# Value and gate products of a two-layer trunk: 256 weight columns a pass at 180 bytes, or 512 at 108 bytes

## The chip, the core and the metric

The kernel runs on one core of a Trainium2 chip. Its time is the device time of one execution in microseconds (us); the time before is the median of three runs. The profile is one further execution, recorded by the hardware profiler. In its rows PE is the matrix engine, PEld the load of its stationary tile, DVE the vector engine, ACT the scalar engine, POOL the general one, SP the engine that issues most transfers.

## The reference

The reference is a trunk of two layers on 256 tokens of width 2048, all in float32:

```python
for i in range(DEPTH):
    h = rms_norm(x, mixer_norm[i])
    if i % N_MIXERS == 0:
        x = x + diff_attention(h, ...)      # h @ w_qkv, scores, softmax, values, @ w_o
    else:
        x = x + gated_deltanet(h, ...)      # h @ w_in, convolution, delta rule, gate z, @ w_out
    x = x + conv_ffn(rms_norm(x, ffn_norm[i]), ...)   # @ w_up, convolution, gate, @ w_down
return x
```

Nearly all of the work is products of 256 tokens with large weights, each weight used once. Two groups of them matter here: the value columns of the attention, `v = h @ w_qkv[:, 4096:6144]`, and the gate columns `z` of the gated DeltaNet, 4096 columns of `h @ w_in`.

## The kernel before

**Three products for one.** Every float32 operand of a large product is split into two parts in the type fp32r, `hi` and the remainder `lo`, and the product is hi·hi + lo·hi + hi·lo, three matmuls accumulated into the same PSUM tile. The activations are kept split in SBUF: `h` holds, for each of the 16 blocks of 128 input features, 256 columns of `hi` and then 256 of `lo`.

**Weights.** `weights` (L78) fetches a piece of 1024 columns, 512 KB, on SP's queue into `raw`, ACT copies it to `whi` (L89), DVE subtracts to get `wlo` (L90). `raw`, `whi` and `wlo` have three buffers each, so a copy to `whi` waits until PE has finished the piece three before. The tiles `whi` and `wlo` are 1024 + 128 elements long, and the second argument of `weights` says at which element of the first 128 the data starts.

**Two kinds of product.** `dense` (L101) has the weight as the stationary tile, 128 x 128, and the activations as the moving one, 256 tokens wide: L115 to L117. It makes 19,344 of the kernel's 23,504 matmuls. `dense_tok` (L125) turns this round, as its result is wanted with the tokens on the partitions: the stationary tile is 128 feature rows by 128 tokens of `h`, the moving one is 512 columns of weight, sent as two halves of 256 (L139). It is called four times with `w_v` (L399) and eight times with `w_z` (L687). Each call goes through 16 blocks `k` of features in 8 pieces of two; for each block it goes over the two halves `c` of the tokens, the three products `j`, and the two halves of the columns: 24 matmuls a piece, 192 a call, 2304 in all. The result has a PSUM tile of two banks, `ps[:, c, :]`, 512 columns each; `dps` holds two such tiles. ACT takes the result out of PSUM, at L402 for v and at L689 for z.

**Placement.** `HP`, `AP`, `OP` are the columns, modulo 128 elements (512 bytes), at which the rows of `h`, of the FFN's activations and of the mixer's output start. `dense` places its weights 45 elements (`GAP`) ahead of that, `dense_tok` 45 elements behind it, so that in both the moving tile starts 180 bytes past the stationary one modulo 512.

**Order.** At the end of each piece `tick` (L73) advances a list of generators by one step each: these do the small work beside the products, such as scores and softmax of the attention during `w_qk` and `w_v`, and during `w_z` the inversion of the delta rule's triangular matrices (`invert`, L512: 30 rounds of two small DVE instructions, L525 and L528, a step each three rounds; then two transposes, L532 and L534, on which PE's L553 waits). `total` (L221) sums squares by a matmul with a tile of ones (L226), with 512 moving columns of fp32r for q and k. The Tile scheduler may move instructions on each engine; each engine then runs its own in order. In layer 1 the calls with `w_z` come in pairs, four pairs in all; `dense` with `w_in` follows each.

Of the kernel before, what the change touches and what calls it, by code (L numbers as in the profile page):

```python
# [16 lines left out]
P = 128  # L17
T = 256
# [1 line left out]
KD = D // P  # L20
EPS = 1e-6
CK = 4
GAP = 45
HP, AP, OP = 40, 48, 112
LNEXP = "natural_log_exp_and_others"

# [1 line left out]
class Trunk:  # L28
# [72 lines left out]
    def dense(self, w, kt, acts, place, tiles=2, lead=0):  # L101
# [3 lines left out]
        for k0, nk in self.chunks(kt, CK, lead):  # L105
            hi, lo = self.weights(w[:, k0:k0 + nk, :], (place - GAP) % P)
            steps = [(k, c) for k in range(nk) for c in range(tiles)]
# [17 lines left out]
    def dense_tok(self, w, kt, acts):  # L125

        nc = self.nc
        ps = self.banks()
        for k0, nk in self.chunks(kt, CK // 2):
            hi, lo = self.weights(w[:, k0:k0 + nk, :], (HP + GAP) % P)  # L130
            for k in range(nk):
                a = acts(k0 + k)
                first, last = k0 + k == 0, k0 + k == kt - 1
                for c in range(2):
                    ah, al = (a[:, i, c * P:(c + 1) * P] for i in range(2))
                    halves = [slice(i * T, (i + 1) * T) for i in range(2)]
                    for j, (l, r) in enumerate(((ah, hi), (ah, lo), (al, hi))):
                        for i, s in enumerate(halves):
                            nc.tensor.matmul(ps[:, c, s], l, r[:, k, s],  # L139
                                             start=first and not (i or j), stop=last and i + j == 3)  # L140
            self.tick()
        return ps

# [764 lines left out]
```

## Time and profile before

| | |
|---|---|
| Median of 3 runs | 2675.52 us (2675.1 to 2675.8) |
| The profiled execution | 2676.33 us, of which its span is 2674.6 us |
| Mean granted clock of TensorE | 0.999 |
| PE, 23,504 matmuls | 2656.4 us busy |
| DVE / ACT / POOL busy | 1845.2 / 1453.3 / 112.1 us |
| HBM read | 476.03 MB, 179 GB/s over the span |

Read it so: a row of the timeline or of a group gives the start in us, the duration, the engine, the line of the kernel, the operation, what it writes and reads, the shape, and how many instructions are merged in it. Matmuls overlap in the pipeline, so the duration of one (some 280 ns for 256 columns) is not what it costs: the cost is the distance from its start to the start of the next. A row x4 at 210.36 followed by a row at 210.84 says that four matmuls cost 0.48 us. A small part of the matmul records can be missing.

### The profile page before, as it was taken

Reading aid. Unit: us, or ns where it says so; the run is one execution under the profiler, and the core shown is the slowest. Engines: PE = TensorE matmul, PEld = TensorE weight load, DVE = VectorE, ACT = ScalarE, POOL = GpSimd, SP = SyncE. Lnnn points to the kernel's source line nnn. Section 1 sums busy time; section 2 is a strip of 40 time slices with the busy share of each in tenths; the row PEclk is TensorE's granted clock in tenths of the full one; section 3 lists DMA queues with packets and bytes.
Section 4 is the critical chain, followed back from the end, with each engine's and each line's share of the span. In section 5 each row is a group of like instructions: output and inputs, shape, how many; then the busy total and the mean of one; then the engine's idle time right before and its main releaser. Section 6 shows DMA issues by size and latency. Waiting matters only on the chain.

```text
span 2674.6 us, 55978 instructions
## 1 busy us (share of the span) xinstructions
PE 2656.4 (99%) x23504; PEld 2639.4 (99%) x23504; DVE 1845.2 (69%) x2719; ACT 1453.3 (54%) x1994; POOL 112.1 (4%) x221
## 2 busy tenths in 40 slices
PE   8999999999999999999999999999999999999999
PEld 8999999999999999999999999999999999999999
DVE  7775567777777555688787687688677777776444
ACT  6555555555555444584764664574565555554333
POOL 0000000000000000031011021021000000000000
PEclk9999999999999999999999999999999999999999
DMA  6555566666666666655355454555466666666765
GB/s 205 172 174 164 159 192 194 195 195 193 195 193 195 193 194 192 190 156 177 115 170 166 143 169 155 157 159 174 143 194 195 194 193 196 193 195 197 203 200 165
DMA packets 135469, 481.77 MB, mean 180 GB/s; under 512 B 15408, under 2 KB 18480, under 8 KB 135216
## 3 DMA queue, kind: packets, MB, share of 16 engines
q1 hardware_dynamic: 134064, 475.58, 58.6%
q8 instruction: 184, 3.01, 0.5%
q10 hardware_dynamic: 1152, 2.61, 0.3%
q14 instruction: 69, 0.57, 0.1%
HBM read 476.03 MB, written 2.10 MB: 179 GB/s over the span
## 4 chain that ended last, share of the span: by engine, by line
PE 93%; DVE 3%; ACT 3%; issue 1%; DMA 1%; ACTq 0%; DVEq 0%; SPq 0%
PE ps L115 26%; PE ps L116 26%; PE ps L117 26%; PE ps L139 10%; PE mp L610 2%; DVE wlo L90 1%; ACT whi L89 1%; PE mp L226 1%; DVE cv L207 1%; ACT L455 0%; PE mp L574 0%; PE mp L580 0%; DMA raw<-w_in 0%; PE mp L589 0%; PE mp L498 0%
## 5 line engine op out<-in xcount | busy, mean ns | idle before, releaser
L90 DVE TENSOR_TENSOR wlo<-raw,whi 128x1024 fp32r<-128x1024 f32 (+2 forms) x909 | 1105.2, 1217 | 660.9 <-ACT whi L89 659.8
L89 ACT CAST whi<-raw 128x1024 fp32r<-128x1024 f32 (+2 forms) x909 | 948.6, 1044 | 1034.8 <-PE ps L117 830.8
L115 PE MATMUL ps<-h,whi 128*128 128x256 f32 x4304 | 1195.0, 278 | 7.8 <-ACT h L152 5.6
L116 PE MATMUL ps<-h,wlo 128*128 128x256 f32 x4304 | 1194.8, 278 | 4.4 <-DVE wlo L90 4.4
L117 PE MATMUL ps<-h,whi 128*128 128x256 f32 x4304 | 1193.7, 277 | 0.0
L115 PEld LDWEIGHTS ps<-h,whi 128*128 128x128 f32 x4304 | 809.4, 188 | 9.8 <-ACT h L152 5.6
L116 PEld LDWEIGHTS ps<-h,wlo 128*128 128x128 f32 x4304 | 809.8, 188 | 7.7 <-DVE wlo L90 5.9
L117 PEld LDWEIGHTS ps<-h,whi 128*128 128x128 f32 x4304 | 810.0, 188 | 0.6
L115 PE MATMUL ps<-ac,whi 128*128 128x256 f32 x1632 | 450.4, 276 | 0.0
L116 PE MATMUL ps<-ac,wlo 128*128 128x256 f32 x1632 | 450.3, 276 | 0.0
L117 PE MATMUL ps<-ac,whi 128*128 128x256 f32 x1632 | 450.2, 276 | 0.0
L115 PEld LDWEIGHTS ps<-ac,whi 128*128 128x128 f32 x1632 | 306.2, 188 | 0.0
L116 PEld LDWEIGHTS ps<-ac,wlo 128*128 128x128 f32 x1632 | 306.2, 188 | 0.0
L117 PEld LDWEIGHTS ps<-ac,whi 128*128 128x128 f32 x1632 | 306.2, 188 | 0.0
L139 PE MATMUL ps<-whi,h 128*128 128x256 f32 x1536 | 251.1, 284 | 0.0
L139 PEld LDWEIGHTS ps<-whi,h 128*128 128x128 f32 x1536 | 213.5, 190 | 0.2
L139 PE MATMUL ps<-wlo,h 128*128 128x256 f32 x768 | 155.7, 284 | 1.0 <-DVE wlo L90 1.0
L115 PE MATMUL ps<-oc,whi 128*128 128x256 f32 x512 | 143.9, 281 | 0.0
L207 DVE SCALAR_TENSOR_TENSOR cv<-u,fcols,cv 128x255 f32<-128x255 f32 (+1 forms) x344 | 142.8, 477 | 0.0
L117 PE MATMUL ps<-oc,whi 128*128 128x256 f32 x512 | 142.5, 278 | 0.0
L116 PE MATMUL ps<-oc,wlo 128*128 128x256 f32 x512 | 142.3, 278 | 0.0
L139 PEld LDWEIGHTS ps<-wlo,h 128*128 128x128 f32 x768 | 119.4, 190 | 2.0 <-DVE wlo L90 1.4
(201 smaller groups left out, 2048.7 us busy)
## 6 DMA issues: line engine op xcount, KB each, us to landing
raw<-w_up SPq DMA_DIRECT2D x344, 512.0 KB, 4.3
raw<-w_down SPq DMA_DIRECT2D x160, 512.0 KB, 4.1
raw<-w_in SPq DMA_DIRECT2D x128, 512.0 KB, 4.1
raw<-w_z SPq DMA_DIRECT2D x64, 512.0 KB, 4.4
raw<-w_out SPq DMA_DIRECT2D x64, 512.0 KB, 3.9
raw<-w_qk SPq DMA_DIRECT2D x63, 512.0 KB, 4.0
raw<-w_v SPq DMA_DIRECT2D x32, 512.0 KB, 3.7
raw<-w_o SPq DMA_DIRECT2D x32, 512.0 KB, 4.1
```

The source lines that it names most:

```text
L89: nc.scalar.copy(hi, raw)
L90: nc.vector.tensor_tensor(lo, raw, hi.bitcast(F32), ALU.subtract)
L115: nc.tensor.matmul(o, hi[:, k, s], a[:, 0, :], start=first, stop=False)
L116: nc.tensor.matmul(o, lo[:, k, s], a[:, 0, :], start=False, stop=False)
L117: nc.tensor.matmul(o, hi[:, k, s], a[:, 1, :], start=False, stop=last)
L139: nc.tensor.matmul(ps[:, c, s], l, r[:, k, s], start=first and not (i or j), stop=last and i + j == 3)
L207: nc.vector.scalar_tensor_tensor(out[:, j:], u[:, :T - j], taps[n - 1 - j], out[:, j:], ALU.mult, ALU.add)
L226: last = self.nc.tensor.matmul(out, self.onesr, p[:, j], start=i + j == 0, stop=i + j == n)
L610: nc.tensor.matmul(p[:, v, :], l(v), r[:, v, :], start=i == 0, stop=i == len(terms) - 1)
```

## The change

`dense_tok` sends the 512 columns of a block in one matmul in place of two. The first and last flags of the accumulation now go by product alone. The data in `whi` and `wlo` starts at element 40 + 27 = 67 in place of 85, so that the moving tile lies 27 elements, 108 bytes, past the stationary tile modulo 512 bytes. The tiles' sizes, the pieces, the transfers, the copies, the ticks and `dense` with its 180 bytes stay as they are.

```diff
-GAP = 45
+GAP, LEAD = 45, 27
...
-            hi, lo = self.weights(w[:, k0:k0 + nk, :], (HP + GAP) % P)
+            hi, lo = self.weights(w[:, k0:k0 + nk, :], HP + LEAD)
             for k in range(nk):
                 a = acts(k0 + k)
                 first, last = k0 + k == 0, k0 + k == kt - 1
                 for c in range(2):
                     ah, al = (a[:, i, c * P:(c + 1) * P] for i in range(2))
-                    halves = [slice(i * T, (i + 1) * T) for i in range(2)]
                     for j, (l, r) in enumerate(((ah, hi), (ah, lo), (al, hi))):
-                        for i, s in enumerate(halves):
-                            nc.tensor.matmul(ps[:, c, s], l, r[:, k, s],
-                                             start=first and not (i or j), stop=last and i + j == 3)
+                        nc.tensor.matmul(ps[:, c, :], l, r[:, k, :], start=first and not j, stop=last and j == 2)
```

## Prediction

> **What bounds the kernel now.** First the page, for its span, its busy engines and the chain that ended last:
>
> ```profile
> span 2674.6 us, 55978 instructions
> ...
> PE 2656.4 (99%) x23504; PEld 2639.4 (99%) x23504; DVE 1845.2 (69%) x2719; ACT 1453.3 (54%) x1994; POOL 112.1 (4%) x221
> ...
> PE 93%; DVE 3%; ACT 3%; issue 1%; DMA 1%; ACTq 0%; DVEq 0%; SPq 0%
> PE ps L115 26%; PE ps L116 26%; PE ps L117 26%; PE ps L139 10%; PE mp L610 2%; DVE wlo L90 1%; ACT whi L89 1%; PE mp L226 1%; DVE cv L207 1%; ACT L455 0%; PE mp L574 0%; PE mp L580 0%; DMA raw<-w_in 0%; PE mp L589 0%; PE mp L498 0%
> ```
>
> PE carries the chain from end to end; the changed line, L139, is 10% of it, about 267 us. Next, who keeps PE waiting:
>
> ```profile
> PE ps L115 <- ACT h L152: 5.6, 1, 5.6
> PE ps L116 <- DVE wlo L90: 4.4, 6, 1.4
> ...
> PE ps L139 <- DVE wlo L90: 1.0, 1, 1.0
> ```
>
> L139 waits 1.0 us in all, and the two rows above it are the largest waits in the kernel. So PE is bound by its own rate, and a nanosecond less for each matmul of L139 comes straight off the end, unless a new wait takes it back. The question is what one matmul costs. The view of line L139, and the timeline of PE, where the distances between starts are what counts:
>
> ```profile
> L139 PEld LDWEIGHTS ps<-whi,h x1536: 186/192/194, 206.3 to 1823.2; 128*128 128x128 f32 x192
> L139 PE MATMUL ps<-whi,h x1536: 278/282/373, 206.4 to 1823.3; 128*128 128x256 f32 x192
> ...
> L139 PE MATMUL ps<-wlo,h x768: 278/285/471, 209.4 to 1823.1; 128*128 128x256 f32 x192
> ...
>   ACT whi L89: 96.4, 64
> ```
>
> ```profile
> 210.12 0.40 PE L139 MATMUL ps<-wlo,h 128*128 128x256 f32 x2
> 210.36 0.64 PE L139 MATMUL ps<-whi,h 128*128 128x256 f32 x4
> ...
> 214.44 0.40 PE L139 MATMUL ps<-wlo,h 128*128 128x256 f32 x2
> 214.68 0.41 PE L139 MATMUL ps<-whi,h 128*128 128x256 f32 x2
> 214.92 0.40 PE L226 MATMUL mp<-sqp,onesr 128*128 128x512 f32 x1
> 215.16 0.28 PE L139 MATMUL ps<-whi,h 128*128 128x256 f32 x1
> 215.27 0.39 PE L226 MATMUL mp<-sqp,onesr 128*128 128x512 f32 x1
> 215.50 0.28 PE L139 MATMUL ps<-whi,h 128*128 128x256 f32 x1
> ```
>
> From 210.12 to 214.44 lie six rounds of six matmuls: 4.32 us / 36 = 120 ns each, so **240 ns for the pair** that makes 512 columns. There are 1536 + 768 = 2304 of them: 2304 x 120 ns = 276 us, which the chain's 10% bears out. Each comes with a load of its own, also 120 ns from one to the next, that takes 192 ns, so every load is under way while the matmul before it streams.
>
> The same view holds the best witness for the new shape: L226 sends 512 columns of the same type in one matmul, 0.24 us before the next start at 214.92, 0.23 us at 215.27. And `dense`, with 256 columns and the same 180 bytes as L139, has two rates:
>
> ```profile
> 1228.83 0.28 PE L115 MATMUL ps<-h,whi 128*128 128x256 f32 x1
> ...
> 1251.86 0.28 PE L115 MATMUL ps<-h,whi 128*128 128x256 f32 x1
> 1252.07 0.69 PE L553 MATMUL mp<-tcc,lt 32*32 32x32 f32 x32
> ...
> 1253.38 0.28 PE L115 MATMUL ps<-h,whi 128*128 128x256 f32 x1
> ...
> 1255.42 0.28 PE L115 MATMUL ps<-h,whi 128*128 128x256 f32 x1
> ```
>
> Directly behind the `w_z` products it runs 64 rounds of three in 23.03 us, 119.9 ns a matmul; after a short break for L553 it runs six rounds in 2.04 us, 113.3 ns. Line, tiles and addresses' rule are the same before and after the break. So the 6.6 ns are no matter of placement alone: PE seems to carry a lag between loads and matmuls along until something lets it catch up. With 256 columns a load has hardly more room than it needs; with 512 it has twice as much.
>
> **The change, part by part.**
>
> *Removed and put in their place:* 1152 matmuls and 1152 stationary loads go, and 1152 matmuls grow from 256 to 512 columns. What does a 512 cost in a row of such? No row shows it, so bounds:
>
> ```profile
> 240.28 0.60 PE L373 MATMUL mp<-aT,v 128*128 128x256 f32 x2
> 240.71 0.38 PE L374 MATMUL mp<-aT,v 128*128 128x128 f32 x2
> ```
>
> ```profile
> L373 PE MATMUL mp<-aT,v x32: 377/379/382, 240.3 to 322.1; 128*128 128x256 f32 x32
> ...
> L374 PE MATMUL mp<-aT,v x32: 271/274/275, 240.7 to 322.4; 128*128 128x128 f32 x32
> ```
>
> ```profile
> 1147.90 0.66 PE L226 MATMUL mp<-qp,onesr 128*128 128x512 f32 x2
> 1148.39 0.29 PE L115 MATMUL ps<-h,whi 128*128 128x256 f32 x1
> ```
>
> Plain float32 takes as long for 128 columns (274 ns) as L139's fp32r for 256 (282 ns), so its 256 columns stand for 512 of fp32r: two of L373 cost 0.43 us, 215 ns each, with a load under each. That is the lower end. The upper end is the slow pair of L226 at 1147.90, 0.49 us for two, 245 ns. The rows between, nearest in kind, are L226's 230 to 240 ns, but those stand alone among 256-column matmuls and lie wherever their tiles happen to. I take 222 ns, half-way between 215 and 230: the load has its room for once, as under L373, but the moving data comes twice as fast as there. Gain: 1152 x (240 - 222) = **20.7 us**; by the ends, 1152 x 25 = 28.8 us gained to 1152 x 5 = 5.8 us lost.
>
> The Trainium skill, page "TensorE: Matmul & The Clock Gate", section "Wait — 56ns, not 53.3ns?", has a warm matmul of N columns cost N / 2.4 GHz and a fixed 2.5 ns or so. By it a 512 would cost 215.8 ns and the sum would be 1152 x 24.2 = 27.9 us; but it also gives 109.2 ns for 256 columns, where the trace has 113.3 and 120, so by the rule alone a pair would save 2.6 ns and the change 3.0 us, an estimate that would be no change, as in the first rival below. The trace speaks against it on the 256.
>
> *The `dense` behind w_z:* four times, once for each pair of calls, some 192 matmuls or more run at 119.9 in place of 113.3 ns: at least 4 x 192 x 6.6 ns = 5.1 us. If the lag is what the halves leave behind, it goes with them. That a 512 lets `dense` fall back to its fast rate is seen here:
>
> ```profile
> 190.04 0.63 PE L226 MATMUL mp<-sqp,onesr 128*128 128x512 f32 x2
> 190.51 0.28 PE L115 MATMUL ps<-h,whi 128*128 128x256 f32 x1
> ...
> 191.55 0.28 PE L115 MATMUL ps<-h,whi 128*128 128x256 f32 x1
> ...
> 195.29 0.28 PE L115 MATMUL ps<-h,whi 128*128 128x256 f32 x1
> ```
>
> After two of them, nine matmuls cost 1.04 us, then 33 cost 3.74 us, 113.3 ns each. I take 3.5 us of the 5.1; the ends are 0 and 5.1.
>
> *The placement* moves the start of the data in `whi` and `wlo` from element 85 to 67. It issues nothing; the two copies write the same 1024 elements into tiles of the same size, so I cost it at nothing on ACT and DVE. Its effect on PE is in the 222.
>
> *Cover.* A piece of 512 KB now lasts 24 x 120 ns = 2.88 us on PE, then 12 x 222 = 2.66 us. Transfers, copies and the ticks' work must fit:
>
> ```profile
> GB/s 205 172 174 164 159 192 194 195 195 193 195 193 195 193 194 192 190 156 177 115 170 166 143 169 155 157 159 174 143 194 195 194 193 196 193 195 197 203 200 165
> ...
> raw<-w_z SPq DMA_DIRECT2D x64, 512.0 KB, 4.4
> ```
>
> ```profile
> 1193.22:1228.83 35.61, 35.61 (x300) 35.61 (x298) 31.32 (x60) 16.64 (x20) 3.22 (x8) 1.00 0.60 191
> ...
> 1787.81:1823.18 35.37, 35.37 (x297) 35.37 (x296) 31.55 (x59) 14.65 (x16) 3.34 (x8) 1.00 0.62 191
> ```
>
> 524 KB in 2.66 us are 197 GB/s, which whole slices of the kernel reach (205, 203); a transfer lands in 4.4 us and has three buffers, 8 us. The windows' figures behind the length are PE, PEld, DVE, ACT and POOL busy. ACT is under half busy, and its copies wait for PE (96.4 us, above). DVE is the tight one: 31.3 of 35.6 us in the long runs of `w_z`, as the inversion runs beside them. PE's time there would shrink by 222/240 to 32.9 us; DVE still fits, with 5% to spare. I take 1 us for waits that appear; the bounds are 0 and the whole gain in `w_z`, 768 x 18 ns = 13.8 us.
>
> **Sum.** 20.7 + 3.5 - 1 = 23.2 us off the profiled execution's 2676.33 us (span 2674.6 and 1.7 around it): 2653.1 us. The median before, 2675.52, is 0.8 us lower, so **2652 us**, 0.9% faster. What is late next is still PE.
>
> **The rivals.**
>
> *The excess goes with the columns, not with the matmul* (no change). Then 512 columns cost 230 to 240 ns, as L226 has them, and the halves were no loss. For it: L226's rows are the only 512s there are. Against it: `dense` at 113.3 and 119.9 ns with one shape. At 235 ns, 1152 x 5 = 5.8 us gained: 2670 us. The Trainium skill, page "SBUF — State Buffer", in its table of the engines' ports, gives PE two independent read ports, one for the moving operand and one for loads, and says that PE waits on nobody; by it 108 or 180 bytes would change nothing. No run here shows either.
>
> *The new placement collides* (slower). In a 512 the load of the next tile reads beside one stream twice as long. If 108 bytes is a bad distance, each pass is held up as L226 is at 1147.90, or more: 250 ns, 10 over the pair, costs 11.5 us, 2687 us. It decides from 240 ns on. For it: that pair's 245 ns. Against it: most rows of L226 lie under 240.
>
> *DVE becomes the bound beside w_z.* Each pair of calls then ends no earlier, or gives the time back at L553, which waits for the inversion: 13.8 us are lost again and about 7 remain, 2668 us. It decides where a piece on PE is shorter than DVE's work for it: 31.5 us in 35.4 us is 2.57 us a piece, 214 ns a matmul, just below the lowest cost that I allow.
>
> **How the numbers follow.** About 0.2% (5.4 us) is what a measurement of this kernel can tell from no change. Forecast 0.60; columns 0.18, of which 0.13 still faster than the bound; collision 0.12, of which 0.02 within it; DVE 0.06, half on each side of it; 0.04 for what I haven't thought of. Faster 0.60 + 0.13 + 0.03 + 0.01 = 0.77, same 0.12, slower 0.11. The range: at the low end 215 ns and the whole 5.1 us, 2675.5 - 33.9 = 2641.6, taken as 2640; the high end takes in the rivals up to no gain at all, 2675, and leaves the collision out.
>
> **What would show it.** In the profile after, 1152 matmuls of 128x512 at L139's place, and the starts of six rounds of three 4.0 us apart (222 ns); at 3.87 us it is the lower end, at 4.2 the columns, above 4.32 the collision. `dense` behind the last `w_z` at 113.3 ns within a dozen matmuls. The list of PE's waits without a new row over 2 us; "L553 <- DVE" or a larger "wlo" in it would be the DVE rival. PE's share of the chain stays at 93%. I am wrong if the 512s run at 235 ns or more, or if the span falls by under 12 us while they run at 222.

## The result, and the profile after

The changed kernel takes 2653.45 us (median of six runs, 2652.38 to 2654.77) against 2675.31 us for the kernel before (six runs): a ratio of 0.9917, 95% interval 0.9905 to 0.993, 0.8% faster. Its profiled execution took 2653.89 us, the span in it 2652.1 us. Three executions among those behind the comparisons below, two of the kernel before and the profiled one of the halves at 0 bytes, took 6309.55 to 7661.13 us and are left out of the ratios.

The page of the changed kernel; its product line is now L137, and the lines behind it have moved up by three (L226 is L223, L553 is L550):

```profile
span 2652.1 us, 53671 instructions
...
PE 2635.5 (99%) x22352; PEld 2573.5 (97%) x22352; DVE 1842.5 (69%) x2719; ACT 1452.8 (55%) x1994; POOL 110.9 (4%) x221
...
PE 96%; ACT 2%; DVE 2%; issue 1%; DMA 0%; SPq 0%; DVEq 0%; ACTq 0%
```

1152 matmuls and as many loads are gone (23,504 to 22,352), and the loads have more idle time (97% busy, where it was 99%). PE still carries the chain, even more of it (96%). What a 512 costs shows in its timeline of PE, in a stretch with nothing between:

```profile
212.11 0.39 PE L137 MATMUL ps<-wlo,h 128*128 128x512 f32 x1
212.34 0.61 PE L137 MATMUL ps<-whi,h 128*128 128x512 f32 x2
...
215.52 0.39 PE L137 MATMUL ps<-wlo,h 128*128 128x512 f32 x1
```

Five rounds of three in 3.41 us: 227 ns a matmul, where two halves took 240. Then `dense` behind the first pair of `w_z` calls:

```profile
1223.93 0.28 PE L115 MATMUL ps<-h,whi 128*128 128x256 f32 x1
...
1249.81 0.28 PE L115 MATMUL ps<-h,whi 128*128 128x256 f32 x1
...
1250.24 0.34 PE L550 MATMUL mp<-tcc,lt 32*32 32x32 f32 x10
```

76 rounds of three in 25.88 us are 113.5 ns a matmul, from the start on; before, this stretch ran at 119.9 ns until L553. The list of PE's waits in the changed kernel, whole:

```profile
PE ps L115 <- ACT h L149: 5.6, 1, 5.6
PE ps L115 <- ACT whi L89: 3.3, 2, 2.4
PE ps L116 <- DVE wlo L90: 3.1, 4, 1.4
PE mp L716 <- DVE glin L712: 0.2, 1, 0.2
PE mp L223 <- ACT qp L215: 0.2, 1, 0.2
```

No matmul of the changed line is in it, nor does L550 wait for DVE. In the windows of a `w_z` stretch (length, then PE, PEld, DVE, ACT, POOL busy) DVE is at 90%, and PEld at 83%, where it was at 100%:

```profile
1193.58:1223.93 30.35, 30.35 (x137) 25.07 (x135) 27.24 (x52) 15.33 (x19) 3.47 (x8) 1.00 0.67 200
```

To see where the 22.5 us of the span went, I add up, over PE's whole timeline, the distance from each start to the next one by the kind of the first matmul:

| us | `dense_tok` | `dense` on h | `dense` on ac, oc | other matmuls | all |
|---|---|---|---|---|---|
| before | 280.8 | 1495.0 | 735.5 | 153.5 | 2664.8 |
| after | 264.4 | 1490.0 | 735.5 | 152.4 | 2642.3 |
| difference | -16.4 | -5.0 | 0.0 | -1.1 | -22.5 |

Three quarters lie in the changed line, nearly all the rest in `dense` on h, which the change does not touch. The 5.0 us there are a net: behind the four pairs of `w_z` calls 863 matmuls of `dense` fall from 103.6 to 98.0 us, 5.6 us, and elsewhere 0.6 us are lost. The same sums are given below for the experiments; each is of one profiled execution.

### The profile page after: what moved, and what is told of

Its sections match the earlier page's. It is cut to its first block, busy times and chain, and to the rows that moved or that the text cites. A ratio compares the mean times of both kernels' runs of the same rounds, so it can differ in the third digit from the quotient of the medians.

```text
span 2652.1 us, 53671 instructions
## 1 busy us (share of the span) xinstructions
PE 2635.5 (99%) x22352; PEld 2573.5 (97%) x22352; DVE 1842.5 (69%) x2719; ACT 1452.8 (55%) x1994; POOL 110.9 (4%) x221
## 3 DMA queue, kind: packets, MB, share of 16 engines
q10 hardware_dynamic: 1152, 2.61, 0.3%
## 4 chain that ended last, share of the span: by engine, by line
PE 96%; ACT 2%; DVE 2%; issue 1%; DMA 0%; SPq 0%; DVEq 0%; ACTq 0%
PE ps L116 27%; PE ps L115 27%; PE ps L117 27%; PE ps L137 10%; PE mp L607 2%; PE mp L223 1%; DVE wlo L90 0%; ACT whi L89 0%; PE mp L495 0%; PE mp L577 0%; PE mp L571 0%; DVE cv L204 0%; PE mp L586 0%; DMA raw<-w_qk 0%; PE mp L651 0%
## 5 line engine op out<-in xcount | busy, mean ns | idle before, releaser
L117 PE MATMUL ps<-h,whi 128*128 128x256 f32 x4304 | 1192.7, 277 | 0.0
L117 PEld LDWEIGHTS ps<-h,whi 128*128 128x128 f32 x4304 | 810.4, 188 | 0.5
L117 PE MATMUL ps<-ac,whi 128*128 128x256 f32 x1632 | 450.2, 276 | 0.0
L117 PEld LDWEIGHTS ps<-ac,whi 128*128 128x128 f32 x1632 | 306.2, 188 | 0.0
L137 PE MATMUL ps<-whi,h 128*128 128x512 f32 x768 | 240.8, 390 | 0.0
L137 PEld LDWEIGHTS ps<-whi,h 128*128 128x128 f32 x768 | 144.1, 188 | 29.8
L137 PE MATMUL ps<-wlo,h 128*128 128x512 f32 x384 | 149.9, 390 | 0.1
L117 PE MATMUL ps<-oc,whi 128*128 128x256 f32 x512 | 142.8, 279 | 0.0
L123 DVE TENSOR_TENSOR u<-ps,rstd 128x512 f32<-128x512 f32 x118 | 81.5, 690 | 38.7 <-PE ps L117 38.3
```

The source lines that it names most:

```text
L117: nc.tensor.matmul(o, hi[:, k, s], a[:, 1, :], start=False, stop=last)
L123: self.nc.vector.tensor_tensor(u, ps[:, :, :T], self.rstd.unsqueeze(1).to_broadcast([P, 2, T]), ALU.mult)
L137: nc.tensor.matmul(ps[:, c, :], l, r[:, k, :], start=first and not j, stop=last and j == 2)
```

## The experiments

The theory in the prediction has two halves: a matmul of 512 columns gives the load of the next tile room that one of 256 does not (the room theory), and PE carries a slow phase from the halves into `dense`. The rival, the placement theory, is that the distance between the moving and the stationary tile makes the difference.

**Size alone, distance alone.** The change has two parts; each is made by itself. First 512 columns at the old distance:

```diff
-GAP, LEAD = 45, 27
+GAP, LEAD = 45, 45
```

> One matmul of 512 columns as in the change, at the old 180 bytes. Room theory (a 256 leaves the load of the next stationary tile next to no room and PE runs with a lag; a 512 has room, whatever the placement): 226 to 230 ns a matmul, 2651 to 2656 us, like the change. Placement theory (the distance of moving and stationary tile modulo 512 bytes sets the cost, and 108 bytes is what the change gains by): 235 to 245 ns, 1152 x 7 to 17 ns more than the change, 2662 to 2673 us.

Measured: 2661.17 us, ratio 0.9951 (0.9934 to 0.9968). Its timeline:

```profile
1214.61 0.40 PE L137 MATMUL ps<-wlo,h 128*128 128x512 f32 x1
1214.84 0.64 PE L137 MATMUL ps<-whi,h 128*128 128x512 f32 x2
...
1218.88 0.40 PE L137 MATMUL ps<-wlo,h 128*128 128x512 f32 x1
```

Six rounds of three in 4.27 us, 237 ns: the distance counts. `dense_tok` sums to 275.1 us, 5.7 below before and 10.7 above the change. `dense` on h is at 1486.3, 8.7 below before.

Then the halves at the new distance:

```diff
-GAP = 45
+GAP, LEAD = 45, 27
...
-            hi, lo = self.weights(w[:, k0:k0 + nk, :], (HP + GAP) % P)
+            hi, lo = self.weights(w[:, k0:k0 + nk, :], HP + LEAD)
```

> Two matmuls of 256 columns as before, at the new 108 bytes. Room theory: 118 to 121 ns a matmul, dense behind w_z still at 120 ns, 2672 to 2677 us, no change from before. Placement theory: the halves fall to the 113.3 ns that dense has, a pair costs 227 ns, and the time is that of the change, 2650 to 2657 us.

Measured: 2668.76 us, ratio 0.9975 (0.9965 to 0.9985). Its timeline, at the end of a pair of `w_z` calls and behind it:

```profile
1223.26 0.40 PE L139 MATMUL ps<-wlo,h 128*128 128x256 f32 x2
1223.50 0.64 PE L139 MATMUL ps<-whi,h 128*128 128x256 f32 x4
...
1226.86 0.40 PE L139 MATMUL ps<-wlo,h 128*128 128x256 f32 x2
...
1227.34 0.28 PE L115 MATMUL ps<-h,whi 128*128 128x256 f32 x1
...
1249.13 0.28 PE L115 MATMUL ps<-h,whi 128*128 128x256 f32 x1
```

The halves stay at 120 ns (five rounds of six in 3.60 us), `dense_tok` at 280.0 us. But `dense` behind them runs 64 rounds in 21.79 us, 113.5 ns. Neither theory had that: nearly the whole gain of this kernel is the 7.5 us that `dense` on h falls by, behind halves that are themselves no faster.

So in `dense_tok` the size alone is worth 5.7 us, the distance alone 0.8, both together 16.4: the two parts of the change work only together. The placement theory was wrong on the halves, the room theory on the 512s.

**Who slows dense down.** Halves in seven pieces of a call, 512 columns in the last, all at 180 bytes:

```diff
-                        for i, s in enumerate(halves):
+                        for i, s in enumerate(halves if k0 + nk < kt else [slice(0, 2 * T)]):
                             nc.tensor.matmul(ps[:, c, s], l, r[:, k, s],
-                                             start=first and not (i or j), stop=last and i + j == 3)
+                                             start=first and not (i or j), stop=last and j == 2)
```

> Halves at 180 bytes in the first seven of the eight pieces of a call, 512 columns in the last piece alone, still at 180 bytes. Room theory: the last piece lets PE catch up, so dense behind w_z runs at 113.3 ns from its start (about 5 us gained in dense) and the last pieces gain 12 x 12 x 12 ns = 1.7 us: 2667 to 2670 us. Placement theory: dense behind w_z stays at 120 ns and the last pieces gain nothing: 2674 to 2677 us.

Measured: 2672.76 us, ratio 0.9991 (0.9981 to 1.0), less than expected. `dense` on h falls by 7.0 us to 1488.0, as the room theory has it, but `dense_tok` rises by 2.1 to 282.9:

```profile
1221.96 0.41 PE L139 MATMUL ps<-wlo,h 128*128 128x256 f32 x2
...
1224.92 0.41 PE L139 MATMUL ps<-wlo,h 128*128 128x256 f32 x2
...
1225.66 0.40 PE L139 MATMUL ps<-wlo,h 128*128 128x512 f32 x1
...
1227.80 0.40 PE L139 MATMUL ps<-wlo,h 128*128 128x512 f32 x1
...
1228.28 0.28 PE L115 MATMUL ps<-h,whi 128*128 128x256 f32 x1
...
1250.05 0.28 PE L115 MATMUL ps<-h,whi 128*128 128x256 f32 x1
```

The halves here cost 2.96 us / 24 = 123 ns, the 512s 2.14 us / 9 = 238 ns, and `dense` 21.77 us / 192 = 113.4 ns. With seven eighths of the halves still there, at the same distance, `dense` is fast. The first call of this pair still has its halves at 120 ns; behind its 512s all 168 halves of the second call run at 123 ns. So the halves have two rates as well: 168 halves 3.3 ns slower are 0.55 us, and as all four pairs show it, these are about the 2.1 us.

A break between the halves and `dense` should do the same, if a phase is carried. The first attempt put four matmuls of 32x32 on the tile of ones behind the loop of `dense_tok`:

```diff
+        gap = self.mp()
+        for _ in range(4):
+            nc.tensor.matmul(gap[:32, :32], self.ones[:, :32], self.ones[:, :32], start=True, stop=True)
         return ps
```

> The kernel before, with four matmuls of 32x32 on a tile of ones behind each of the twelve calls (their output is not used). If PE carries a slow phase from the halves into dense and a short break ends it, as L553 does: dense behind w_z at 113.3 ns, 5 to 8 us less in dense, the halves unchanged at 120 ns, some 2 us for the added matmuls: 2669 to 2673 us. If the slow stretch belongs to the stage (its traffic, its engines): no gain, 2675 to 2678 us.

Measured: 2681.86 us, ratio 1.0024 (1.0014 to 1.0034). It tells nothing on `dense`: nothing depends on the result of the added matmuls, so the scheduler may move them. In the first pair those of the first call stayed between the two calls (1210.17 us); those of the second landed at 1271.82 us, far inside `dense`, behind the first matmuls of the line that is L553 in the kernel before. `dense` behind `w_z` stayed at 120.0 ns, with no break ahead of it. The halves behind the break at 1210.17 ran at 120 ns, as before. The added work cost 6.5 us (others +3.3 us, `dense_tok` +1.6, `dense` on h +1.6).

The second attempt ties the break to its place, as it adds zeros to the result itself:

```diff
+        self.zero = self.cp.tile([P, P], F32, tag="zero", name="zero")
+        nc.vector.memset(self.zero, 0.0)
...
-                                             start=first and not (i or j), stop=last and i + j == 3)
+                                             start=first and not (i or j), stop=False)
             self.tick()
+        for c in range(2):
+            nc.tensor.matmul(ps[:, c, :32], self.zero, self.zero[:, :32], start=False, stop=True)
```

> The kernel before, with two plain float32 matmuls of 32 columns of zeros added to the result at the end of each of the twelve calls, so that they stand between the last half and the next product (in the run before with added matmuls the scheduler moved them elsewhere, and the 192 matmuls of dense behind w_z stayed at 119.9 ns). If PE carries a slow phase from the halves into dense and a break ends it: dense behind w_z at 113.3 ns, 5 to 8 us less there, some 1.5 us for the added matmuls, 2668 to 2672 us. If the slow stretch belongs to the stage: 2675 to 2679 us.

Measured: 2674.52 us, ratio 0.9997 (0.9987 to 1.0006). Its timeline (L145 is the break, L141 the halves, L117 the first line of `dense`; a plain float32 matmul shows as two):

```profile
1208.47 0.41 PE L141 MATMUL ps<-wlo,h 128*128 128x256 f32 x2
...
1231.41 0.41 PE L141 MATMUL ps<-wlo,h 128*128 128x256 f32 x2
1231.65 0.41 PE L141 MATMUL ps<-whi,h 128*128 128x256 f32 x2
1231.90 0.53 PE L145 MATMUL ps<-zero 128*128 128x32 f32 x4
1232.26 0.37 PE L117 MATMUL ps<-h,whi 128*128 128x256 f32 x1
...
1232.70 0.28 PE L117 MATMUL ps<-h,whi 128*128 128x256 f32 x1
...
1250.04 0.28 PE L117 MATMUL ps<-h,whi 128*128 128x256 f32 x1
```

51 rounds in 17.34 us: 113.3 ns. `dense` on h sums to 1488.9 us, 6.1 less. The break's own cost (others +3.9 us, `dense_tok` +1.9) eats this up, so the total lies above the 2668 to 2672 us expected and is no better than before. That the slow stretch belongs to the stage is ruled out, by this run as by the halves at 108 bytes and by the 512s in the last piece, all with `dense` at 113.3 to 113.5 ns in the same place. That the break alone ended a phase is less sure, because the halves ahead of it are not as they were: behind the first call's break, from 1208.47 to 1231.41, 31 rounds of six cost 22.94 us, 123.3 ns in place of 120. Halves at 123 ns may leave nothing behind, and a break can put a stream into a slow rate as well as out of it.

**Without halves.** The kernel before and the changed kernel, in the same stretch of `dense` on h. The last matmuls of `dense_tok` lie over 850 us back:

```profile
1170.49 0.73 PE L226 MATMUL mp<-qp,onesr 128*128 128x512 f32 x2
1171.06 0.28 PE L116 MATMUL ps<-h,wlo 128*128 128x256 f32 x1
...
1175.94 0.28 PE L117 MATMUL ps<-h,whi 128*128 128x256 f32 x1
```

```profile
1168.29 0.73 PE L223 MATMUL mp<-qp,onesr 128*128 128x512 f32 x2
1168.86 0.28 PE L116 MATMUL ps<-h,wlo 128*128 128x256 f32 x1
...
1174.02 0.28 PE L117 MATMUL ps<-h,whi 128*128 128x256 f32 x1
```

The same 43 matmuls behind the same pair cost 4.88 us, 113.5 ns, before and 5.16 us, 120.0 ns, after. With the break at the end, `dense` runs at 120.0 ns from 1124.08 to 1141.00 us (141 matmuls), also ahead of all `w_z` calls; in the kernel before this stretch is at 113.3 ns. So the slow phase comes without halves too, and halves are one way into it, not its only cause. Nor does it need a break to end. In the kernel before, behind the second pair:

```profile
1399.23 0.28 PE L115 MATMUL ps<-h,whi 128*128 128x256 f32 x1
...
1433.78 0.28 PE L115 MATMUL ps<-oc,whi 128*128 128x256 f32 x1
...
1435.49 0.28 PE L115 MATMUL ps<-oc,whi 128*128 128x256 f32 x1
```

`dense` on h takes 34.55 us for 288 matmuls, 120.0 ns; at the first matmul with the moving tile oc, with nothing between, the rate is 1.71 us / 15 = 114 ns. What the runs show is that one stream can have two rates and keeps the one it started with until something changes; which one it starts with, they do not explain.

**The distance for 512 columns.** At 0, 256 and 352 bytes; the edit is that for 0 bytes, with 64 and 88 elements in the two others (at 88 the start is taken as `(HP + LEAD) % P`, which is 0):

```diff
-GAP, LEAD = 45, 27
+GAP, LEAD = 45, 0
```

> 512 columns, the moving tile at the same place modulo 512 bytes as the stationary tile. Room theory: 226 to 232 ns, 2651 to 2658 us, as placement counts for little. Placement theory: a worse distance than 180 bytes, 240 ns or more a matmul, 2668 us or more.

> 512 columns at 256 bytes. So far a 512 costs 228 ns at 0 and 108 bytes and 237 ns at 180. Window theory (only a band of distances around 180 bytes holds up the stream): 227 to 230 ns, 2649 to 2655 us. Slope theory (the further the moving tile starts past the stationary one, the more the load and the stream meet): 240 ns or more, 2664 us or more.

> 512 columns at 352 bytes, where the moving tile starts at a multiple of 512 bytes. Window theory: 227 to 230 ns, 2649 to 2655 us. Slope theory: 245 ns or more, 2670 us or more. [...]

Measured at 0 bytes: 2650.79 us, ratio 0.9907 (0.9893 to 0.9922); at 256: 2652.07 us, 0.9912 (0.9896 to 0.9929); at 352: 2656.5 us, 0.9931 (0.9916 to 0.9946). The timelines at 0, at 256 and at 352 bytes:

```profile
1213.76 0.39 PE L137 MATMUL ps<-wlo,h 128*128 128x512 f32 x1
...
1217.84 0.39 PE L137 MATMUL ps<-wlo,h 128*128 128x512 f32 x1
```

```profile
1213.69 0.39 PE L137 MATMUL ps<-wlo,h 128*128 128x512 f32 x1
...
1217.77 0.39 PE L137 MATMUL ps<-wlo,h 128*128 128x512 f32 x1
```

```profile
1213.90 0.39 PE L137 MATMUL ps<-wlo,h 128*128 128x512 f32 x1
...
1217.40 0.39 PE L137 MATMUL ps<-wlo,h 128*128 128x512 f32 x1
```

Six rounds in 4.08 us are 226.7 ns at 0 and at 256 bytes, five in 3.50 us are 233.3 ns at 352. `dense_tok` sums to 264.6 us (0 bytes), 264.4 (108), 275.1 (180), 264.1 (256) and 270.5 (352). The slope theory falls at 256 bytes, the theory of one band around 180 at 352; what rule the distances follow stays open. In all these runs h stays where it is and only the weights move, so a rule that goes by the start of the moving tile alone would fit as well as one that goes by the distance; that was not tried. Nothing was gained by a start at a multiple of 512 bytes. The kernels at 0 and 256 bytes are a little below the change, but their intervals overlap its own, and the difference from it at 0 bytes, 2.7 us, lies in `dense` on h (1487.0 against 1490.0); a version that is clearly better than the change was not found.

**Can halves be fast?** At 0 bytes and, with 64 elements, at 256, edited as the halves at 108 bytes were; and in another order at 180 bytes:

```diff
-GAP = 45
+GAP, LEAD = 45, 0
```

```diff
-                    for j, (l, r) in enumerate(((ah, hi), (ah, lo), (al, hi))):
-                        for i, s in enumerate(halves):
+                    for i, s in enumerate(halves):
+                        for j, (l, r) in enumerate(((ah, hi), (ah, lo), (al, hi))):
```

> Two halves of 256 columns, at 0 bytes. If halves can be as fast as a 512 at some distance: 113 to 115 ns a half, 227 to 230 ns a pair, 2650 to 2656 us, and the size of the matmul counts for nothing. If a half leaves the load too little room wherever it lies: 118 to 122 ns, 2666 to 2676 us, as at 108 and 180 bytes.

> Two halves of 256 columns at 256 bytes, a distance at which one matmul of 512 costs 227 ns. If a half leaves the load too little room at any distance: 118 to 122 ns, 2666 to 2676 us. If the good distances of the 512 are good for halves as well: 113 to 115 ns, 2650 to 2656 us.

> The halves of before at 180 bytes, with the three products inside each half: the same matmuls and loads in the order that dense has, in place of the two halves of a product one behind the other with the same stationary tile. If the order of the loads makes the halves slow: 113 to 115 ns a matmul, 227 to 230 ns a pair, 2650 to 2658 us. If it does not: 119 to 121 ns, 2668 to 2677 us, according to whether dense behind w_z is fast or slow.

Measured: at 0 bytes 2669.85 us, ratio 0.9978 (0.9968 to 0.9987), of which I have the time alone; at 256 bytes 2669.83 us, 0.9975 (0.9966 to 0.9985); in the other order 2676.6 us, 1.0002 (0.9993 to 1.0012). At 256 bytes:

```profile
1220.27 0.40 PE L139 MATMUL ps<-wlo,h 128*128 128x256 f32 x2
...
1223.87 0.40 PE L139 MATMUL ps<-wlo,h 128*128 128x256 f32 x2
```

Five rounds of six in 3.60 us: 120 ns again, and `dense_tok` 279.8 us; `dense` behind it runs 192 matmuls at 113.4 ns. In the other order the halves are at 120 ns, too, and `dense` behind `w_z` stays at 120.0. So the halves cost 120 ns at each of the three distances and in both of the orders whose timelines I have. Behind all four pairs, `dense` is slow where the halves lie at 180 bytes, in either order, and fast where they lie at 108 or 256.

**Does dense care about the distance?** The changed kernel, with `dense` at 108 bytes as well:

```diff
-GAP, LEAD = 45, 27
+GAP, LEAD = 27, 27
```

> The changed kernel with dense, too, at 108 bytes (its weights 27 elements ahead of the activations in place of 45). If the distance holds up only streams of 512 columns, as the halves at 0, 108, 180 and 256 bytes suggest (119 to 121 ns at each): dense stays at 113.3 ns, 2650 to 2656 us, and one distance would serve both products. If a 256 in its fast phase depends on the distance as a 512 does: dense at 116 to 120 ns in the 19,344 matmuls, 52 to 130 us more, 2700 to 2785 us.

Measured: 2712.28 us, ratio to the kernel before 1.0137 (1.012 to 1.0154). The same stretch of the FFN, first in the changed kernel, then in this one:

```profile
640.13 0.28 PE L115 MATMUL ps<-h,whi 128*128 128x256 f32 x1
...
642.17 0.28 PE L115 MATMUL ps<-h,whi 128*128 128x256 f32 x1
```

```profile
640.09 0.28 PE L115 MATMUL ps<-h,whi 128*128 128x256 f32 x1
...
642.19 0.28 PE L115 MATMUL ps<-h,whi 128*128 128x256 f32 x1
```

Eighteen matmuls take 2.10 in place of 2.04 us, 116.7 in place of 113.3 ns. In the sums over all 19,344 matmuls of `dense` the difference is 57.6 us, nearly the 58.8 us between the medians of this kernel and of the change; `dense_tok` keeps its 264.4. The distance that is good for 512 columns in `dense_tok` is a poor one for 256 in `dense`. The expectation that distance counts for the 512s alone was wrong.

## Why the prediction was right, and where it was not

*PE is the bound, and a nanosecond saved in L139 comes off the end.* Right: 22.5 us fewer in PE's sum, 22.5 us fewer in the span.

*The 512s, 20.7 us.* Right in sign, too large: 16.4 us. A 512 came out at 227 ns where I took 222; with all that stands between, 264.4 us / 1152 = 229.5 ns for a 512 and 280.8 / 1152 = 243.7 for a pair of halves, 14.2 ns apart in place of 18. The mis-sized number is the midpoint between 215 and 230: plain float32 turned out no guide (the two L373 of 215 ns are one matmul, which shows as two), and L226, the row nearest in kind, with its 230 ns, was nearly right. At the three good distances a 512 costs 226.7 or 227 ns, just twice the 113.3 ns of `dense`. The Trainium skill's rule in "TensorE: Matmul & The Clock Gate", section "Wait — 56ns, not 53.3ns?", would have it at 215.8; the lowest here is 226.7.

*The placement, counted inside the 222.* Mis-sized in kind: it is no detail of that number. At the old distance a 512 costs 237 ns, and of the 16.4 us only 5.7 would have come; 10.7 hang on the 108 bytes. The rule of the Trainium skill, page "SBUF — State Buffer", section "Who interferes with whom", that PE waits on nobody and that its two read ports are independent, would have both alike. The runs at 180 bytes (237 against 227 ns) and with `dense` at 108 (116.7 against 113.3 ns) show that placement counts; that the ports are the reason is not shown.

*Dense behind w_z, 3.5 us of 0 to 5.1.* Right in its place and sign, and larger: 5.6 us behind the four pairs, above the upper end, as one of the stretches has 288 matmuls and not 192; 5.0 us net in `dense` on h (4 to 9 in the other kernels in which it happened). That PE carries a rate along is borne out, by the 288 matmuls at 120.0 ns and by the 512s in the last piece. That "it goes with the halves" was half of the cause: halves at 108 or 256 bytes do not leave it behind, and it comes where no halves are. That two 512s let `dense` fall back to its fast rate, read at 190.51, is no rule: behind the pair at 1168.29 of the changed kernel it stays at 120.0 ns. The 5.6 us came back, but that they would was in part luck, as the runs give no rule for when a stream is slow. That halves are slow because the load has next to no room is not shown by any run: `dense` has the same room and is at 113.3 ns, and in `dense_tok` no distance or order that I tried made halves fast. What else sets the two apart, such as which operand lies where, was not tried and stays open.

*Waits, 1 us lost.* None appeared, and 1.1 us were gained in the other matmuls. DVE was at 90% in the `w_z` window and PE did not wait for it. The sums make 16.4 + 5.0 + 1.1 = 22.5 us in place of 23.2: an over- and two under-estimates, which nearly cancel.

*The rivals.* "The excess goes with the columns" is right about the best case of each shape (226.7 = 2 x 113.3 ns), and wrong for the halves as they stood at 120. A placement that slows the 512s exists, but at 180 and 352 bytes, not at 108, and even at 180 it leaves a 512 just below its two halves. The DVE rival did not come.

## What to carry to other kernels

Where PE is the bound and its matmuls stand back to back, read the distance between starts: here a stream of the same shape cost 113, 117, 120 or 123 ns a matmul, and neither the durations, all near 280 ns, nor the busy share showed it. The placement of the tiles, which was varied here within 512 bytes, has to be tried for each product by itself: the 108 bytes that are good for 512 columns in `dense_tok` cost the 256 of `dense` 3%, and the 180 bytes that are good there cost the 512s 5%. A stream elsewhere can change its rate with the one that was changed, so compare the others, too.

## What the runs showed of the hardware that was not expected

A stream of 512 columns of fp32r cost 226.7 ns at 0, 108 (227 in its stretch) and 256 bytes, 237 ns at 180 and 233 ns at 352: good and bad placements alternate. A stream keeps its rate for long: `dense` on h stayed at 120.0 ns through 288 matmuls (34.55 us), and halves at 123.3 ns through a whole call behind two float32 matmuls of zeros that took 0.37 us. The same 43 matmuls behind the same pair of 512s ran at 113.5 ns in one kernel and at 120.0 in the other.
